# Output projection: where the first half's last twelve products stand among the second half's

## The chip, the cores and the metric

The kernel runs on one core of one Trainium2 chip. The time is the device time of one execution in microseconds, the median of three runs. Five engines work side by side, each through its own queue in order: TensorE (PE, the matrix products; its weight loads are shown apart as PEld), VectorE (DVE), ScalarE (ACT), GpSimd (POOL) and SyncE (SP, which here only issues DMAs).

## What is computed

One decoder block on 512 tokens of width 1024, in float32: a gated merge of an attention and a pooling branch, projected back by `w_out`, then an MLP. The part that matters here, cut from the reference:

```python
merged = gates[:, :, 0] * a + gates[:, :, 1] * p
x = x + (merged @ w_out[l]).astype(x.dtype)
h2 = rmsnorm(x, norm_mlp_g[l])
z = jnp.square(jax.nn.relu(h2 @ w_up[l]))
x = x + (z @ w_down[l]).astype(x.dtype)
```

## The kernel before

Every float32 product is made of three faster ones. A matrix is split into a high part (a rounded copy, written by ACT, line 112 for weights) and a low part (the difference, written by DVE, line 113), and high x high, high x low and low x high are summed in PSUM. So each weight tile costs a cast on ACT, then a subtract on DVE, before all its products can run.

The output projection takes `merged` (high part `vh`, low part `vl` in the profile, `mh` and `ml` in the code, in 8 slices `k` of 128 columns) times `w_out`, in two halves of 512 output columns. Each half has four weight tiles, and each tile serves two slices `k`. They are called o0_0 to o0_3 for the first half and o1_0 to o1_3 for the second; `wh_` and `wl_` are their high and low parts. The tokens are four row tiles of 128. A product of row tile t and slice k is three PE instructions of shape 128x512 (lines 588, 589, 590): `vh` x `wh`, `vh` x `wl`, `vl` x `wh`. Row tile t of the first half sums in PSUM bank po0_t, of the second half in po1_t. The profile drops the numbers and calls all of them po, wh_o, wl_o.

The high parts lie in a rotation of four buffers, so the high part of o1_3 goes where that of o0_3 was: its cast waits until the last product that reads o0_3 is done. Those products (slice k = 7 of the first half, twelve instructions) need the merge of the last attention head, which comes late. The low parts lie in four buffers of their own.

When a bank is complete, DVE adds it to the residual `x1` (line 594) and ACT sums the squares of the row (line 568). After the second half's add, a short chain on ACT and DVE (lines 578 to 582) makes the row's scale, line 645 writes the normalised row tile `h2`, and eight PE transposes (line 653) bring it into the layout of the up projection (banks h2T*t*). Their banks are split again into high and low (lines 665 and 666, tiles gab1 and gab2), which the first products of the up projection (lines 792, 795 and 798, banks um) read.

The kernel is written with a tile framework that orders the instructions of each engine itself: it runs its own cost model while it builds the program, and takes next what it reckons is ready. `after(later, earlier)` adds a rule of order without a semaphore: `later` may not be placed ahead of `earlier`. Without a rule, products of different banks may be mixed.

Of the kernel before, what the change touches and what calls it, by code (L numbers as in the profile page):

```python
# [21 lines left out]
NK = D // P  # L22
# [29 lines left out]
def block_kernel(ctx, tc, xT, x_tok, gains, pos, consts, w_in, w_v, w_pool, w_out, w_up, w_dn, out):  # L52
# [4 lines left out]
    def after(later, earlier):  # L57
        tc.add_manual_dep(
            later.ins, earlier.ins.name,
            mybir.DependencyInfo(mybir.DependencyClass.NoSync, mybir.DependencyReason.DATA), reason="issue order",  # L60
        )

    state = {}
# [8 lines left out]
    def bank(i, name):  # L72
        return ps.tile([P, S], F32, tag=f"b{i}", name=name)
# [16 lines left out]
    def f(ap):  # L90
        return ap.bitcast(F32)
# [24 lines left out]
    def get_w(src, name, eng=None, hold=None):  # L116
        raw, hi, lo = load_w(src, name)
        if eng == "dma":

            A.copy(out=hi, in_=raw)  # L120
            A.mul(out=lo, in_=f(hi), mul=-1.0)
            G.dma_start(out=lo, in_=src, accum_op=ALU.add)
        else:
            ins = split_w(raw, hi, lo, eng=eng)
            if hold:
                after(ins, hold)
        return hi, lo
# [91 lines left out]
    for n in range(2):  # L219
        accs = [bank((0, 1, 2, 3, 4, 5, 6, 0)[4 * n + t], f"v{n}_{t}") for t in range(NT)]  # L220
        for kk in range(4):
# [7 lines left out]
            for k2 in range(2):  # L229
# [4 lines left out]
                k = 2 * kk + k2  # L234
# [327 lines left out]
    def gain(g, i):  # L562
        nc.sync.dma_start(out=g, in_=gains[i])
        return g, A.mul(out=g, in_=g, mul=-0.5)
# [10 lines left out]
    def row_scale(t, n):  # L575

        src, r, u = (st[:, t, i : i + 1] for i in (n, 4, 5))
        A.activation(out=r, in_=src, func=AF.Ln, scale=1.0 / D, bias=st[:, t, 2:3])
        A.activation(out=r, in_=r, func=AF.Exp, scale=-0.5)
        state["rows"] = A.activation(out=u, in_=r, func=AF.Square, scale=1.0 / math.sqrt(D))  # L580
        V.scalar_tensor_tensor(out=u, in0=src, scalar=st[:, t, 3:4], in1=u, op0=ALU.add, op1=ALU.mult)
        V.scalar_tensor_tensor(out=r, in0=u, scalar=-3.0, in1=r, op0=ALU.add, op1=ALU.mult)
        return r

    def mm_rows(a_, t, k, w, start, stop):
        hi, lo = w
        sl, tsl = slice((k % 2) * 512, (k % 2) * 512 + 512), slice(t * P, t * P + P)
        m = T.matmul(a_, lhsT=mh[:, k, tsl], rhs=hi[:, sl], start=start, stop=False)
        T.matmul(a_, lhsT=mh[:, k, tsl], rhs=lo[:, sl], start=False, stop=False)
        return m, T.matmul(a_, lhsT=ml[:, k, tsl], rhs=hi[:, sl], start=False, stop=stop)  # L590

    def x1_add(t, n, a_):
        xs = x1[:, t, n * 512 : n * 512 + 512]
        V.tensor_tensor(out=xs, in0=a_, in1=xs, op=ALU.add)
        return square(t, n, R[t][:, 0:2, :].rearrange("p a t -> p (a t)"))

    def forms_h2(forms, x):

        w, u, a11, a12 = (h_[:, i, :, x] for h_ in (hw, h2f) for i in range(2))
        for form in forms:  # L600
            ins = None
            if form in (S2, S4):
                ins = V.scalar_tensor_tensor(out=w, in0=w, scalar=-1.0, in1=a11 if form == S2 else a12, op0=ALU.mult, op1=ALU.subtract)
            elif form == S3:
                ins = V.tensor_tensor(out=u, in0=a11, in1=u, op=ALU.subtract)
            if form in (S3, S4):
                after(ins, state[form - 1])
            hi, lo = (g_[:, :, x] for g_ in gf[form])
            A.copy(out=hi, in_=u if form == S3 else w)
            state[form] = V.tensor_tensor(out=lo, in0=u if form == S3 else w, in1=f(hi), op=ALU.subtract)  # L610

    po = [bank(t, f"po0_{t}") for t in range(NT)]
    for kk in range(4):
        w = get_w(w_out[0, kk], f"o0_{kk}", V if kk else "dma", state["scaled"] if kk > 1 else None)
        for k in (2 * kk, 2 * kk + 1):
            for t in range(NT):
                m, _ = mm_rows(po[t], t, k, w, k == 0, k == NK - 1)
                if k == 4:
                    after(m, state["pv"])
    for t in range(NT):  # L620
# [5 lines left out]
    g2b, _ = gain(R[4].rearrange("p b c -> p (b c)"), 0)  # L626
# [7 lines left out]
    for t in range(NT):  # L634
        a_ = bank(4 + t, f"po1_{t}")
        for k in range(NK):
            m, end = mm_rows(a_, t, k, ws[k // 2], k == 0, k == NK - 1)
            if t > 1 and k == 0:
                after(m, state["po"])
        if 0 < t < 3:  # L640
            for b in range(2):
                after(state["h2T", t - 1, b], end)
        state["po"] = end
        x1_add(t, 1, a_)
        state["h2", t] = V.scalar_tensor_tensor(out=h2[:, t % 2], in0=x1[:, t, :], scalar=row_scale(t, 1), in1=g2b, op0=ALU.mult, op1=ALU.mult)
        pv = []
        for b in range(2):
            pt = bank((t % 2) * 2 + b, f"h2T{t}_{b}")
            for j in range(4):
                k = 4 * b + j  # L650
                if j == 1:
                    state["h2T", t, b] = state["h2T"]
                state["h2T"] = T.transpose(out=pt[:, j * P : j * P + P], in_=h2[:, t % 2, k * P : k * P + P], identity=ident)
            pv.append(pt.rearrange("p (j q) -> p j q", q=P))
        sl = slice((t % 2) * P, (t % 2) * P + P)
        if t > 1:

            A.copy(out=hw[:, 1, :, sl], in_=pv[0])
            V.tensor_tensor(out=hw[:, 0, :, sl], in0=pv[1], in1=hw[:, 1, :, sl], op=ALU.subtract)
            forms_h2((S1, S2), sl)  # L660
        if t == 3:
            forms_h2((S3,), slice(0, HS))
        for b in range(t // 2, 2):
            hi, lo = (gab[b][:, t // 2, i, :, sl] for i in range(2))
            A.copy(out=hi, in_=pv[b])
            part = V.tensor_tensor(out=lo, in0=pv[b], in1=f(hi), op=ALU.subtract)
            if t == 3:
                after(part, state[S3])
            if t < 2:
                A.copy(out=h2f[:, b, :, sl], in_=pv[b])  # L670
# [371 lines left out]
```

## Time and profile before

| | |
|---|---|
| median of three runs | 672.47 us (672.26 to 672.51) |
| the profiled execution, its own time | 672.8 us |
| its span, first to last instruction | 671.0 us |
| so outside the span | 1.8 us |
| PE busy | 661.8 us, 99% of the span |
| DVE busy | 529.6 us, 79% |
| ACT busy | 467.5 us, 70% |
| PE's share of the chain of waits that ended last | 98% |

The output projection's products run from 297 to 348 us of the span, and the up projection follows at once. In the timeline, a row is a start in us, a duration in us, the engine and line, output <- inputs, a count, and in brackets the idle time ahead of it with what ended it. The end of a product is modelled: a 128x512 product shows 0.39 us, but the next one starts before that. "xN" at a row's end means N instructions merged, and the duration is then of all of them.

### The profile page before, as it was taken

Reading aid. Unit: us, or ns where it says so; the run is one execution under the profiler, and the core shown is the slowest. Engines: PE = TensorE matmul, PEld = TensorE weight load, DVE = VectorE, ACT = ScalarE, POOL = GpSimd, SP = SyncE. Lnnn points to the kernel's source line nnn. Section 1 sums busy time; section 2 is a strip of 40 time slices with the busy share of each in tenths; the row PEclk is TensorE's granted clock in tenths of the full one; section 3 lists DMA queues with packets and bytes.
Section 4 is the critical chain, followed back from the end, with each engine's and each line's share of the span. In section 5 each row is a group of like instructions: output and inputs, shape, how many; then the busy total and the mean of one; then the engine's idle time right before and its main releaser. Section 6 shows DMA issues by size and latency. Waiting matters only on the chain.

```text
span 671.0 us, 9986 instructions
## 1 busy us (share of the span) xinstructions
PE 661.8 (99%) x3680; PEld 578.3 (86%) x3680; DVE 529.6 (79%) x897; ACT 467.5 (70%) x756; POOL 91.1 (14%) x115
## 2 busy tenths in 40 slices
PE   9999999999999999999999999999999999999995
PEld 7888888888888888888789988999889998899884
DVE  6855977799979978795688999658993599747995
ACT  8465587979788688976477974368743695266974
POOL 2001110021012112300202020202102021211120
PEclk9999999999999999999999999999999999999998
DMA  9416474345254357454876596876959588584863
GB/s 320 155 60 188 123 153 126 87 123 113 95 133 127 95 132 151 104 174 178 283 203 115 165 228 184 174 207 132 235 195 194 183 163 260 132 199 135 211 126 126
DMA packets 32737, 108.82 MB, mean 162 GB/s; under 512 B 4016, under 2 KB 4912, under 8 KB 32688
## 3 DMA queue, kind: packets, MB, share of 16 engines
q0 software_dynamic: 10512, 38.28, 32.0%
q1 hardware_dynamic: 21744, 69.38, 29.4%
q8 instruction: 29, 0.48, 0.3%
q10 hardware_dynamic: 432, 0.52, 0.2%
q14 instruction: 20, 0.16, 0.1%
HBM read 106.07 MB, written 2.10 MB: 161 GB/s over the span
## 4 chain that ended last, share of the span: by engine, by line
PE 98%; DMA 1%; DVE 0%; ACT 0%; issue 0%; SPq 0%
PE um L795 8%; PE um L792 8%; PE um L798 8%; PE dm L885 8%; PE dm L887 8%; PE dm L888 8%; PE v L237 2%; PE o L420 2%; PE ga L134 2%; PE ga L133 2%; PE k L137 2%; PE ga L137 2%; PE gp L137 2%; PE k L134 2%; PE k L133 2%; PE gp L134 2%
## 5 line engine op out<-in xcount | busy, mean ns | idle before, releaser
L403 ACT ACTIVATE p<-p,st 128x128 f32<-128x128 f32 (+3 forms) x64 | 35.8, 561 | 19.8 <-DVE st L399 19.5
L887 PE MATMUL dm<-wh_dt,z 128*128 128x512 f32 (+1 forms) x128 | 49.5, 387 | 0.0
L888 PE MATMUL dm<-wl_dt,z 128*128 128x512 f32 (+1 forms) x128 | 49.4, 386 | 0.0
L885 PE MATMUL dm<-wh_dt,z 128*128 128x512 f32 (+1 forms) x128 | 49.0, 387 | 0.0
L795 PE MATMUL um<-gss,wh_ut 128*128 128x256 f32 x192 | 48.2, 283 | 0.0
L792 PE MATMUL um<-gss,wh_ut 128*128 128x256 f32 x192 | 48.0, 283 | 0.0
L905 DVE TENSOR_TENSOR x<-x,dm 128x512 f32<-128x512 f32 x48 | 32.5, 681 | 15.7 <-PE dm L888 15.6
L112 ACT CAST wh_ut<-wga_uNone 128x1024 fp32r<-128x1024 f32 x24 | 24.8, 1051 | 28.5 <-PE dm L887 19.9
L112 ACT CAST wh_ub<-wr_u 128x1024 fp32r<-128x1024 f32 x24 | 25.1, 1049 | 25.4 <-PE um L795 10.7
L113 DVE TENSOR_TENSOR wl_ut<-wga_uNone,wh_ut 128x1024 fp32r<-128x1024 f32 x24 | 29.0, 1221 | 12.7 <-ACT wh_ut L112 12.7
L887 PE MATMUL dm<-wh_db,z 128*128 128x512 f32 x96 | 37.2, 389 | 0.0
L888 PE MATMUL dm<-wl_db,z 128*128 128x512 f32 x96 | 37.2, 389 | 0.0
L795 PEld LDWEIGHTS um<-gss,wh_ut 128*128 128x128 f32 x192 | 36.9, 192 | 0.0
L792 PEld LDWEIGHTS um<-gss,wh_ut 128*128 128x128 f32 x192 | 36.8, 192 | 0.0
L885 PE MATMUL dm<-wh_db,z 128*128 128x512 f32 x96 | 35.7, 389 | 0.0
L113 DVE TENSOR_TENSOR wl_ub<-wr_u,wh_ub 128x1024 fp32r<-128x1024 f32 x24 | 29.1, 1219 | 8.4 <-ACT wh_ub L112 8.4
L112 ACT CAST wh_dt<-wga_dNone 128x1024 fp32r<-128x1024 f32 x24 | 24.9, 1050 | 14.9 <-issue 6.9
L694 POOL DMA_DIRECT2D wga_dNone<-w_dn x16 | 13.9, 868 | 154.2 <-DVE wl_dt L113 154.2
L765 DVE TENSOR_TENSOR z<-rawz,z 128x1024 fp32r<-128x1024 f32 x28 | 33.6, 1216 | 0.5 <-ACT z L762 0.5
L399 DVE CUSTOM_DVE_ANT_0 p<-s,mask 128x128 f32<-128x128 f32 (+3 forms) x64 | 30.6, 482 | 3.2 <-PE s L398 3.0
L795 PE MATMUL um<-gab,wh_ub 128*128 128x256 f32 x128 | 32.5, 283 | 0.0
L792 PE MATMUL um<-gab,wh_ub 128*128 128x256 f32 x128 | 32.4, 283 | 0.0
(322 smaller groups left out, 2174.4 us busy)
## 6 DMA issues: line engine op xcount, KB each, us to landing
wr_u<-w_up SPq DMA_DIRECT2D x24, 512.0 KB, 5.7
wr_d<-w_dn SPq DMA_DIRECT2D x24, 512.0 KB, 4.1
wga_uNone<-w_up POOLq DMA_DIRECT2D x18, 512.0 KB, 6.1
wga_dNone<-w_dn POOLq DMA_DIRECT2D x16, 512.0 KB, 5.7
wr_k<-w_in SPq DMA_DIRECT2D x8, 512.0 KB, 3.3
wr_ga<-w_in SPq DMA_DIRECT2D x8, 512.0 KB, 3.3
wr_gp<-w_in SPq DMA_DIRECT2D x8, 512.0 KB, 3.4
wl_ga<-w_in POOLq DMA_DIRECT2D x8, 512.0 KB, 5.4
```

The source lines that it names most:

```text
L112: ins = A.copy(out=hi[:, sl], in_=raw[:, sl])
L113: state["low"] = (eng or G).tensor_tensor(out=lo[:, sl], in0=raw[:, sl], in1=f(hi)[:, sl], op=ALU.subtract)
L134: T.matmul(acc, lhsT=hi[:, c], rhs=rl[k], start=False, stop=False)
L137: T.matmul(acc, lhsT=lo[:, c], rhs=rh[:, k, :], start=False, stop=k == NK - 1)
L403: A.activation(out=pr[:, c, :N], in_=pr[:, c, :N], func=AF.Exp, scale=-1.0, bias=st[:, c : c + 1], accum_out=st[:, 2 + c : 3 + c])
L765: lo = V.tensor_tensor(out=z[:, 1], in0=r, in1=f(z[:, 0]), op=ALU.subtract)
L792: m = T.matmul(a_, lhsT=hi[:, c], rhs=rh[:, k, :], start=p + k == 0 and onto is None, stop=False, skip_group_check=True)
L795: T.matmul(a_, lhsT=hi[:, c], rhs=rl[:, k, :], start=False, stop=False, skip_group_check=True)
L798: m = T.matmul(a_, lhsT=lo[:, c], rhs=rh[:, k, :], start=False, stop=k == 3, skip_group_check=True)
L885: m = T.matmul(a_, lhsT=zh, rhs=hi[:, sl], start=p == 0 and start, stop=False, skip_group_check=True)
L887: T.matmul(a_, lhsT=zl, rhs=hi[:, sl], start=False, stop=False, skip_group_check=True)
L888: end = T.matmul(a_, lhsT=zh, rhs=lo[:, sl], start=False, stop=p == 3, skip_group_check=True)
```

## The change

Two lines of order. `state["po"]` now holds, once the first half is written, the last product of its last bank. In the second half, row tile 0 may not begin slice k = 6 (the first that reads weight tile o1_3) until that product is placed. And the products of row tiles 1, 2 and 3 start only after those of the row tile ahead of them have all been placed; before, this held for row tiles 2 and 3 alone.

```diff
@@ -614,7 +614,7 @@
         w = get_w(w_out[0, kk], f"o0_{kk}", V if kk else "dma", state["scaled"] if kk > 1 else None)
         for k in (2 * kk, 2 * kk + 1):
             for t in range(NT):
-                m, _ = mm_rows(po[t], t, k, w, k == 0, k == NK - 1)
+                m, state["po"] = mm_rows(po[t], t, k, w, k == 0, k == NK - 1)
                 if k == 4:
                     after(m, state["pv"])
     for t in range(NT):
@@ -635,7 +635,7 @@
         a_ = bank(4 + t, f"po1_{t}")
         for k in range(NK):
             m, end = mm_rows(a_, t, k, ws[k // 2], k == 0, k == NK - 1)
-            if t > 1 and k == 0:
+            if t and k == 0 or not t and k == NK - 2:
                 after(m, state["po"])
         if 0 < t < 3:
             for b in range(2):
```

What this does to the order of PE around the end of the first half, first as it was. (In these rows po0 and po1 are the banks of the two halves, then the row tile; wh_o1_3 is the high part of the second half's last weight tile.)

```order
L589 MATMUL po0_3_3007<-wl_o0_3_3102,vh_113 128x512
L590 MATMUL po0_3_3007<-wh_o0_3_3101,vl_114 128x512
L590 MATMUL po1_1_3224<-wh_o1_1_3159,vl_114 128x512
L588 MATMUL po1_1_3224<-wh_o1_2_3165,vh_113 128x512
L589 MATMUL po1_1_3224<-wl_o1_2_3166,vh_113 128x512
L590 MATMUL po1_1_3224<-wh_o1_2_3165,vl_114 128x512
L588 MATMUL po1_1_3224<-wh_o1_2_3165,vh_113 128x512
L589 MATMUL po1_1_3224<-wl_o1_2_3166,vh_113 128x512
L590 MATMUL po1_1_3224<-wh_o1_2_3165,vl_114 128x512
L588 MATMUL po1_0_3175<-wh_o1_3_3171,vh_113 128x512
L588 MATMUL po1_1_3224<-wh_o1_3_3171,vh_113 128x512
L589 MATMUL po1_0_3175<-wl_o1_3_3172,vh_113 128x512
```

The first two rows end the first half. Seven products of row tile 1 stand between them and the first that reads o1_3, and two high-part products before the first that reads its low part. Ahead of these rows, 18 products of row tile 0 and 11 of row tile 1 stood mixed with the first half's last twelve: 41 products in all, up to and with the second row.

The same place now:

```order
L588 MATMUL po0_2_3006<-wh_o0_3_3101,vh_113 128x512
L589 MATMUL po0_2_3006<-wl_o0_3_3102,vh_113 128x512
L588 MATMUL po0_3_3007<-wh_o0_3_3101,vh_113 128x512
L589 MATMUL po0_3_3007<-wl_o0_3_3102,vh_113 128x512
L590 MATMUL po0_0_3004<-wh_o0_3_3101,vl_114 128x512
L590 MATMUL po0_1_3005<-wh_o0_3_3101,vl_114 128x512
L590 MATMUL po0_2_3006<-wh_o0_3_3101,vl_114 128x512
L590 MATMUL po0_3_3007<-wh_o0_3_3101,vl_114 128x512
L588 MATMUL po1_0_3175<-wh_o1_3_3171,vh_113 128x512
L589 MATMUL po1_0_3175<-wl_o1_3_3172,vh_113 128x512
L590 MATMUL po1_0_3175<-wh_o1_3_3171,vl_114 128x512
```

The twelve now follow the 18 products of row tile 0 directly (30 products up to the last of the first half, so it stands 11 earlier), their four `vl` products come together at the end, and the very next product reads o1_3. All 11 products of row tile 1 have moved behind row tile 0, with the rest of their row tile.

On DVE, the place at which the low part of o1_3 is made reads the same in both kernels:

```order
L594 TENSOR_TENSOR x1_2994<-po0_0_3004,x1_2994 128x512
L594 TENSOR_TENSOR x1_2994<-po0_1_3005,x1_2994 128x512
L594 TENSOR_TENSOR x1_2994<-po0_2_3006,x1_2994 128x512
L594 TENSOR_TENSOR x1_2994<-po0_3_3007,x1_2994 128x512
L113 TENSOR_TENSOR wl_o1_3_3172<-wr_o1_3_3169,wh_o1_3_3171 128x1024
L572 TENSOR_SCALAR st2_3003<-st2_3003 128x1
```

Nothing moved here: the subtract stands behind the four adds of the first half's banks.

Later on PE, a piece of the difference among row tile 2's products (the transposes of row tile 0's `h2`):

```order
 L589 MATMUL po1_2_3273<-wl_o1_2_3166,vh_113 128x512
 L590 MATMUL po1_2_3273<-wh_o1_2_3165,vl_114 128x512
+L653 MATMUL h2T0_0_3208<-ident_87,h2_2996 128x128 x4
+L653 MATMUL h2T0_1_3213<-ident_87,h2_2996 128x128 x4
 L588 MATMUL po1_2_3273<-wh_o1_3_3171,vh_113 128x512
 L589 MATMUL po1_2_3273<-wl_o1_3_3172,vh_113 128x512
```

Row tile 0's transposes moved forward by 19 places, from among row tile 3's products. Those of row tiles 1, 2 and 3 keep their place to within four rows. On ACT and DVE the chains of row tile 0 and row tile 1 (lines 568 to 645), which were interleaved, now stand one behind the other. No instruction is added or removed on any engine, and the orders of POOL and SP are unchanged.

## The prediction

> **What bounds the kernel now.** I read the page first (busy shares, the chain that ended last), then PE's waits over the whole run, then the timeline around the end of the first half. The page:
>
> ```profile
> span 671.0 us, 9986 instructions
> PE 661.8 (99%) x3680; PEld 578.3 (86%) x3680; DVE 529.6 (79%) x897; ACT 467.5 (70%) x756; POOL 91.1 (14%) x115
> PE 98%; DMA 1%; DVE 0%; ACT 0%; issue 0%; SPq 0%
> ```
>
> The waits of PE, in us, times, longest:
>
> ```profile
> PE warm L172 <- POOL eps L163: 1.1, 1, 1.1
> PE po L589 <- DVE wl_o L113: 0.4, 1, 0.4
> PE v L237 <- ACT wh_v L112: 0.3, 1, 0.3
> ```
>
> PE is the bound from end to end, and it idles three times. One idle, 0.4 us, is at the place of the change: the product that needs the low part of o1_3. So whatever makes PE wait here is paid in full at the end, for behind this place PE never waits and can give nothing back; and no new order can win more here than that wait.
>
> PE around it (a pair merged at 329.90: the last product of the first half, then one of row tile 1):
>
> ```profile
> 329.90 0.62 PE L590 MATMUL po<-wh_o,vl 128*128 128x512 f32 x2
> ...
> 331.71 0.61 PE L588 MATMUL po<-wh_o,vh 128*128 128x512 f32 x2
> 332.69 0.50 PE L589 MATMUL po<-wl_o,vh 128*128 128x512 f32 x1 [0.37 <-DVE wl_o L113]
> 333.03 0.40 PE L590 MATMUL po<-wh_o,vl 128*128 128x512 f32 x1
> ...
> 335.09 0.39 PE L588 MATMUL po<-wh_o,vh 128*128 128x512 f32 x1
> ...
> 342.35 0.39 PE L590 MATMUL po<-wh_o,vl 128*128 128x512 f32 x1
> ```
>
> The last two rows are the first and last of 33 in a row: 7.26 us / 32 = 0.227 us a product. ACT and DVE there:
>
> ```profile
> 325.43 1.06 ACT L564 ACTIVATE rawz<-rawz 128x1024 f32<-128x1024 f32 x1 [0.39 <-DMA rawz<-gains]
> 330.32 1.06 ACT L112 CAST wh_o<-wr_o 128x1024 fp32r<-128x1024 f32 x1 [3.83 <-PE po L590]
> 328.51 2.51 DVE L594 TENSOR_TENSOR x<-po,x 128x512 f32<-128x512 f32 x4 [2.22 <-PE po L590]
> 331.41 1.23 DVE L113 TENSOR_TENSOR wl_o<-wr_o,wh_o 128x1024 fp32r<-128x1024 f32 x1 [0.40 <-ACT wh_o L112]
> ```
>
> This is a chain: the first half's last product ends (329.90 + 0.39 = 330.29), the cast of o1_3 starts 0.03 later and ends at 331.38, the subtract ends at 332.64, the product starts at 332.69. From end of product to next product 2.40 us; nine products of the second half ran meanwhile, and hid all but the tail.
>
> **The change part by part.** *The wait that goes.* Behind the pair at 331.71 the next product was due at 331.71 + 2 x 0.227 = 332.16; it came at 332.69 (0.53 late), and the one behind it after 0.34 instead of 0.227 (0.11 more). Cost of the old wait: 0.64 us.
>
> *The wait that comes.* By the order, the last product of the first half stands 11 places earlier: 329.90 - 11 x 0.227 = 327.40, ending at 327.79. Nothing holds it up on the way: the last `vl` it reads is written at 323.33 (the row below), 3.4 us before its first use.
>
> ```profile
> 322.64 0.69 DVE L497 TENSOR_TENSOR vl<-o,vh 128x512 fp32r<-128x512 f32 x1 [0.69 <-ACT vh L496]
> 319.40 1.22 DVE L113 TENSOR_TENSOR wl_o<-wr_o,wh_o 128x1024 fp32r<-128x1024 f32 x1
> 320.54 0.68 DVE L484 TENSOR_TENSOR o<-o,y 128x512 f32<-128x512 f32 x1
> 345.88 1.88 DVE L666 TENSOR_TENSOR gab<-h2T,gab 128x512 fp32r<-128x512 f32 x3
> ```
>
> ACT is free from 326.49 (the 325.43 row), so the cast runs 327.82 to 328.88. All of the cover is gone: the next product reads this cast and the one after it the subtract, and behind these two on PE's queue stands everything else. The subtract has a second condition: it stands behind four adds, which are now released nearly together. The first add's product starts three steps before 327.40 and ends at 327.11, so it starts at 327.14 (0.03 later, as 328.51 followed a product's end). DVE instructions of this size follow one another every 0.60 us (the 345.88 row: 1.88 for three of 0.68 each), so the fourth starts at 328.94 and ends at 329.62. The next starts 0.08 before such an end (319.40 + 1.22 against 320.54): 329.54. The subtract ends at 330.77, and the L589 product starts 0.05 later, at 330.82. It was due at 327.40 + 2 x 0.227 = 327.85: 2.97 late, with the slow restart (0.11) 3.08 us. The profile would show this as about 1.1 us idle before L588 and 1.5 before L589.
>
> The sum: 3.08 - 0.64 = **+2.44 us**.
>
> *Bounds of that term.* Below: if the adds did not delay the subtract (it would start at 328.91 and end at 330.14), the product starts at 330.19, 2.34 late: 2.34 + 0.11 - 0.64 = +1.81. Above: if the adds run one behind the other without overlap (0.69 each, as the single rows show), +0.09 x 3 = +2.71. I take 2.44, since DVE rows of this size do follow at 0.60.
>
> *What moves behind the wait.* All later PE work shifts by 2.44 us, and so must what feeds it, or a second wait appears. The moved transposes of row tile 0 need its `h2`. The chain from a row tile's add to its `h2`, alone in the queues:
>
> ```profile
> 348.41 0.68 DVE L594 TENSOR_TENSOR x<-po,x 128x512 f32<-128x512 f32 x1
> 349.19 1.29 DVE L645 SCALAR_TENSOR_TENSOR h<-x,st,rawz 128x1024 f32<-128x1024 f32 x1
> 351.12 1.28 DVE L645 SCALAR_TENSOR_TENSOR h<-x,st,rawz 128x1024 f32<-128x1024 f32 x1
> ```
>
> The last row is row tile 3's: 351.12 + 1.28 - 348.41 = 3.99 us (349.19 is row tile 2's, used further down). Bank po1_0 is now complete five products into the restart, 330.82 + 0.11 + 4 x 0.227 + 0.39 = 332.2; plus 3.99 and one 1.05 us weight cast that now stands in the chain on ACT: 337.3. The transposes come 47 products after that L589, at 341.6: a margin of 4.3 us. Row tile 1's bank is complete at 337.7, its `h2` at 341.7, its transposes at 347.0. Costed at nothing. Tighter is the low part of `h2` for the up projection's first products:
>
> ```profile
> 345.29 1.03 PE L653 MATMUL h2T<-ident,h 128*128 128x128 f32 x8
> 347.88 0.31 PE L795 MATMUL um<-gab,wh_ub 128*128 128x256 f32 x1
> 353.06 1.03 PE L653 MATMUL h2T<-ident,h 128*128 128x128 f32 x8
> 391.35 1.21 DVE L765 TENSOR_TENSOR z<-rawz,z 128x1024 fp32r<-128x1024 f32 x1
> 395.29 0.62 PE L885 MATMUL dm<-wh_dt,z 128*128 128x512 f32 x2
> ```
>
> Today the third L666 ends at 345.88 + 1.88 = 347.76, 0.12 before L795 reads it. After the change, three more products stand between row tile 1's transposes and L795 (about 3.3 us instead of 2.59), so this margin widens to some 0.7, unless DVE is behind a weight subtract. Costed at nothing, with its price below. Row tile 2's transposes have 2.6 us of room today (353.06 - 350.48), and its chain shifts with PE. Much later the order swaps a weight subtract (1.14 us) with the split of `z`: today that split ends at 392.56, and the first product of that `z` starts at 395.29, so 1.6 us remain. Costed at nothing. The earlier `h2` of row tile 0 gains nothing either: PE never waited for it.
>
> The span becomes 671.0 + 2.44 = 673.4, the profiled time 672.8 + 2.44 = 675.2; the median stands 0.3 below that execution, so 672.47 + 2.44 = **674.9 us**, 0.36% more. Three runs span 0.25 us; under 0.2% (1.3 us) a difference counts as none.
>
> **The rivals.** *Not slower: the cover remains.* The releaser of the cast is inferred. If its buffer were free before the twelve end, and the subtract not behind the adds, only ACT would hold it: cast from 326.49, subtract done at 326.49 + 1.06 + 0.03 + 1.23 = 328.81, product at 328.86, 1.01 late: 1.01 + 0.11 - 0.64 = +0.5, 672.9. It decides if the cast begins by 326.5. For it: only that releasers are inferred. Against: 0.03 us between product's end and cast, and the adds ahead on DVE's queue. Faster than 671.8 (no wait at all, -0.64) has no source, as PE idles nowhere else behind.
>
> *A second wait at L795.* If one weight subtract (1.14 us pitch, 320.54 - 319.40) slips in ahead of row tile 1's L666, 0.7 of margin leaves 0.4 to 0.5 of wait: 675.4.
>
> *The clock falls in the pause.* The granted clock, in windows of 1 us at the end (last columns: PEclk, DMA share, GB/s), PE's last product being over at 663.6:
>
> ```profile
> 666.00:667.00 1.00, 0.00 (x0) 0.00 (x0) 0.65 (x1) 0.64 (x2) 0.00 (x0) 1.00 0.72 281
> 667.00:668.00 1.00, 0.00 (x0) 0.00 (x0) 0.00 (x0) 0.00 (x0) 0.00 (x0) 0.57 0.98 373
> 668.00:669.00 1.00, 0.00 (x0) 0.00 (x0) 0.00 (x0) 0.00 (x0) 0.00 (x0) 0.50 0.95 369
> ```
>
> It halves some 3.5 us into idleness. The new pause has two idle pieces of 1.1 and 1.5 us with a product between, so the clock should stay at 1.00. If it fell all the same, and for as long as it took to fall, 3.5 us at half rate lose 1.75: 674.9 + 1.75 = 676.7. The Trainium skill (TensorE: Matmul & The Clock Gate, Part 1: The HAM clock gate) says that a whole free-running window of about 3.4 us without work drops the array's clock to half, and a busy one restores it. By that rule nothing is added here, and one window lost would cost an estimated 1.7 us, 676.6. The windows above agree with it.
>
> **How the numbers follow.** The forecast, a pause between the bounds (+1.81 to +2.71): 0.78. Second wait: 0.07. Clock: 0.05. Cover remains: 0.05. A mishap that I don't see, of either sign: 0.05. Slower: 0.78 + 0.07 + 0.05 + 0.01 = 0.91; same 0.05 + 0.02 = 0.07; faster 0.02. The range runs from 674.3 (lower bound) less 0.1 for the spread of runs to the second wait on the upper bound, 672.47 + 2.71 + 0.5 = 675.7, plus 0.1: 674.2 to 675.8; it leaves out cover and clock.
>
> **What would show it.** Right: the cast of o1_3 near 327.8; PE idle for o1_3 in two pieces, 2.6 us in all instead of 0.37; the subtract starting right behind the fourth add, 0.6 us after the cast is done; row tile 0's transposes without a wait; PEclk 1.00 from 330 to 336; PE's sum of busy time unchanged. Wrong: the cast starting before the fourth `vl` product ends (cover), a PE wait on L795 or L653 (second wait), a product pitch above 0.227 behind the pause (clock), or less than 2 us of idle time with a span that grows all the same.

## The result, and the profile after

The median of six executions is 677.0 us (674.6 to 679.1), against 672.7 us (672.3 to 673.7) for six of the kernel before on the same chip. The ratio is 1.0057, with a 95% interval of 1.0046 to 1.0069. The change is slower, as forecast; but by 4.3 us, where 2.4 were forecast, and outside the range. The six times are also far apart: 674.61 and 675.40 on one side, 676.72, 677.29, 677.43 and 679.14 on the other. The first two show a mean granted clock of 0.998 over the execution, the others 0.993 to 0.995.

The profiled execution is the 679.14 us one. First two lines of its page and the two waits of PE that the change concerns (us, times, longest):

```profile
span 677.3 us, 9984 instructions
PE 665.4 (98%) x3680; PEld 580.6 (86%) x3680; DVE 529.6 (78%) x897; ACT 468.7 (69%) x756; POOL 91.3 (13%) x115
...
PE po L589 <- DVE wl_o L113: 1.4, 1, 1.4
...
PE po L588 <- ACT wh_o L112: 1.1, 1, 1.1
```

The pause has come as forecast, in two pieces of 1.1 and 1.4 us. But PE's busy time has also grown, from 661.8 to 665.4 us, with the same 3680 products: some of them ran longer. The timeline of PE (start, duration in us) shows which:

```profile
328.98 1.07 PE L590 MATMUL po<-wh_o,vl 128*128 128x512 f32 x4
331.19 0.50 PE L588 MATMUL po<-wh_o,vh 128*128 128x512 f32 x1 [1.14 <-ACT wh_o L112]
333.08 0.51 PE L589 MATMUL po<-wl_o,vh 128*128 128x512 f32 x1 [1.39 <-DVE wl_o L113]
...
333.88 0.59 PE L589 MATMUL po<-wl_o,vh 128*128 128x512 f32 x1
334.26 0.63 PE L590 MATMUL po<-wh_o,vl 128*128 128x512 f32 x1
...
337.25 0.43 PE L588 MATMUL po<-wh_o,vh 128*128 128x512 f32 x1
```

(This execution began 2.2 us late, which is taken up at the end; all times here are later by that.) From 334.26 to 337.25 the products follow at 0.427 us instead of 0.227. The granted clock, in windows of 1 us (last three columns: PEclk, DMA share, GB/s), says why:

```profile
333.00:334.00 1.00, 0.92 (x4) 0.79 (x5) 0.61 (x9) 0.60 (x2) 0.26 (x2) 0.96 0.85 246
334.00:335.00 1.00, 1.00 (x4) 0.81 (x3) 0.07 (x1) 0.00 (x0) 0.71 (x1) 0.50 1.02 205
...
337.00:338.00 1.00, 1.00 (x6) 0.78 (x5) 0.00 (x0) 1.00 (x2) 0.00 (x0) 0.84 1.04 274
...
671.00:672.00 1.00, 0.00 (x0) 0.00 (x0) 0.55 (x2) 0.94 (x4) 0.00 (x0) 0.92 0.02 8
```

A window of 1 us at 0.96 was at half rate for 0.08 us, so the clock fell at 333.92; 0.84 means 0.32 us, so it was back at 337.32, 3.40 us later. The last row is the kernel's end, where PE has nothing more to do: the clock falls there at 671.84. ACT and DVE in the pause:

```profile
330.09 1.05 ACT L112 CAST wh_o<-wr_o 128x1024 fp32r<-128x1024 f32 x1 [1.36 <-PE po L590]
329.41 2.48 DVE L594 TENSOR_TENSOR x<-po,x 128x512 f32<-128x512 f32 x4 [0.89 <-PE po L590]
331.81 1.22 DVE L113 TENSOR_TENSOR wl_o<-wr_o,wh_o 128x1024 fp32r<-128x1024 f32 x1
```

The cast starts as the last product of the first half is done, and the subtract 0.08 us before the fourth add ends, 0.67 us after the cast. That is the chain that was forecast.

### The profile page after: what moved, and what is told of

The parts are those of the page before. It is cut to its first block, busy times and chain, and to the rows that moved or that the text cites. A ratio compares the mean times of both kernels' runs of the same rounds, so it can differ in the third digit from the quotient of the medians.

```text
span 677.3 us, 9984 instructions
## 1 busy us (share of the span) xinstructions
PE 665.4 (98%) x3680; PEld 580.6 (86%) x3680; DVE 529.6 (78%) x897; ACT 468.7 (69%) x756; POOL 91.3 (13%) x115
## 4 chain that ended last, share of the span: by engine, by line
PE 96%; DMA 1%; DVE 1%; ACT 0%; SPq 0%; issue 0%
PE um L798 8%; PE um L795 8%; PE um L792 8%; PE dm L885 7%; PE dm L887 7%; PE dm L888 7%; PE v L237 2%; PE v L238 2%; PE o L420 2%; PE v L239 2%; PE ga L134 2%; PE ga L133 2%; PE k L137 2%; PE ga L137 2%; PE gp L137 2%; PE k L134 2%
## 5 line engine op out<-in xcount | busy, mean ns | idle before, releaser
L795 PE MATMUL um<-gss,wh_ut 128*128 128x256 f32 x192 | 48.2, 283 | 0.0
L795 PEld LDWEIGHTS um<-gss,wh_ut 128*128 128x128 f32 x192 | 36.9, 192 | 0.0
L795 PE MATMUL um<-gab,wh_ub 128*128 128x256 f32 x128 | 32.5, 283 | 0.0
```

Source lines behind the costliest of these rows:

```text
L795: T.matmul(a_, lhsT=hi[:, c], rhs=rl[:, k, :], start=False, stop=False, skip_group_check=True)
```

## The experiments

**Theory A.** The change costs the pause (+2.4 us), and in most executions, on top of it, a stretch at half clock that the pause sets off. **Theory B.** The clock's fall in this one profile is incidental; the time beyond +2.4 us comes from elsewhere, such as the start of the execution.

Of the change's two rules the second alone (row tile 1 behind row tile 0) gives every engine the order of the changed kernel, and the first alone (slice 6 of row tile 0 behind the first half) leaves the old order; so the two were not run apart.

### The changed kernel again

No edit.

> The changed kernel once more, for the spread of its time. Theory A (the clock falls in the pause of some executions): two kinds of execution, about 675.0 us with a mean granted clock of 0.998 and about 677.2 with 0.994 or 0.995, the second in about two of three. Theory B (the time beyond +2.44 us comes from the start of an execution, where the first weights landed 0.6 us later in the profiled one): times spread between 674.6 and 679.2 without a second value of the clock that goes with them.

The ratio is 1.0052 (1.0039 to 1.0065). Two executions with a clock of 0.998 took 674.71 and 675.38 us; four with 0.991 to 0.995 took 676.94, 676.95, 676.98 and 678.18. The second value of the clock goes with the longer time in every one of them, which speaks for A. It does not yet say which causes which.

### The pause kept, but filled

```diff
+            if not t and k == NK - 2:
+                fill, prev = bank(7, "fill"), state["po"]
+                for _ in range(5):
+                    d = T.matmul(fill, lhsT=mh[:, 0, 0:P], rhs=ws[0][0][:, 0:512], start=True, stop=True)
+                    after(d, prev)
+                    prev = d
...
+                m = T.matmul(a_, lhsT=mh[:, k, 0:P], rhs=hi[:, 0:512], start=False, stop=False)
...
+                for _ in range(6):
...
-            if t and k == 0 or not t and k == NK - 2:
+            if t and k == 0:
```

> The changed kernel with eleven extra products in the pause: five before the product that waits for the cast of o1_3 and six between it and the product that waits for the subtract. They write a bank whose content is then overwritten. Eleven times 0.227 us is 2.5 us, as long as the pause, so PE is busy there but the cast and the subtract come no earlier. Theory A: the pause's 2.44 us stay, the clock doesn't fall: 674.9 us (674.4 to 675.4) in every execution, clock 0.998. Theory B: the spread is as in the changed kernel, median near 677, up to 679.

The eleven extra products land in the pause, and the chain behind it keeps its times. PE, then ACT and DVE:

```profile
326.60 1.07 PE L590 MATMUL po<-wh_o,vl 128*128 128x512 f32 x4
327.51 1.29 PE L640 MATMUL fill<-wh_o,vh 128*128 128x512 f32 x5
328.82 0.50 PE L644 MATMUL po<-wh_o,vh 128*128 128x512 f32 x1
329.15 1.56 PE L648 MATMUL fill<-wh_o,vh 128*128 128x512 f32 x6
330.70 0.51 PE L651 MATMUL po<-wl_o,vh 128*128 128x512 f32 x1
327.71 1.05 ACT L112 CAST wh_o<-wr_o 128x1024 fp32r<-128x1024 f32 x1 [1.39 <-PE po L590]
329.43 1.22 DVE L113 TENSOR_TENSOR wl_o<-wr_o,wh_o 128x1024 fp32r<-128x1024 f32 x1
```

The product that waits for the subtract starts 4.10 us after the four-product row, as in the changed kernel (333.08 - 328.98). All five executions lie between 674.97 and 675.82 us; the median is 675.15, against 676.94 for the changed kernel on the same chip. Eleven products of useless work make the kernel 1.8 us faster, because PE is not idle. Theory B would have left the spread. (The mean clock of four of the five is 0.996, and that value alone marks no fall in the pause: the half clock behind PE's last product counts in it too. In the first profile after the change, 5.5 us of it there (671.84 to 677.3) and 3.4 us at the pause make 1 - 0.5 x 8.9 / 677.3 = 0.993. Only the 675.15 us execution was profiled; its clock reads 1.00 around the pause.) What stays, 675.15 against 673.07 of the kernel before, is the pause, 2.1 us by these medians.

### Only the first piece filled

The same edit with the six products left out.

> The changed kernel with five of the extra products only, ahead of the product that waits for the cast. One idle piece of 1.4 us is left in front of the product that waits for the subtract. The fall of the clock by a share of idleness in a window of 3.41 us (falls were seen at 2.0 us and more idle in one window, none at 1.47): no fall, 675.0 us (674.5 to 675.6) in every execution. If any idle piece of over 1 us can set the fall off, wherever it lies: about 676.7 in more than half of the executions.

The five executions took 674.64 to 676.08 us, median 675.45, and the profile (the 675.01 us one) shows 1.4 us of idleness at that product and a clock of 1.00 throughout. There, one piece of 1.4 us set nothing off. The two longest, 675.72 and 676.08, lie above what was expected and were not profiled. The kernel before alone ranged from 672.29 to 674.19 here, but a fall in these two is not ruled out.

### A longer pause

```diff
         split_w(raw, hi, lo)
+        if kk == 3:
+            V.tensor_tensor(out=lo, in0=raw, in1=f(hi), op=ALU.subtract)
```

> The changed kernel with the subtract that makes the low part of o1_3 done a second time; the second product of o1_3 waits for that one, which stands behind six short instructions of DVE: the second idle piece grows from 1.4 to about 2.9 us. Theory A: now every position of the windows has one with 2 us idle, so all executions lie in one group: 675.0 + 1.5 + 1.2 to 1.7 for the half rate (less where part of that window is idle) = 677.7 to 678.3, and none near 676.5. If the fall hangs on something else than the idle time, two groups stay, 676.5 and 678.2.

One group, as A has it, though higher than expected: 679.39, 679.61 and 679.65 us, and one of 681.16. PE's waits:

```profile
PE po L589 <- DVE wl_o L632: 2.9, 1, 2.9
...
PE po L588 <- ACT wh_o L112: 1.1, 1, 1.1
```

The second piece is the 2.9 us that was expected. Of the 1.3 us that the estimate missed, 0.4 is a new wait of PE far behind (`PE um L794 <- ACT rawz L822`), and 0.6 lies behind PE's last product; I did not follow these further. By the mean clocks, 0.992 to 0.995, no execution escaped the half clock; only the 679.61 us one was profiled. Four are few: if nine in fifteen fall, as they do without this edit, four in a row come by chance once in eight times. The 681.16 us execution, at 0.992, stays unexplained.

### Where the fall is decided: three more profiles

No edit.

> The changed kernel, one profile more, for the place of the windows. The falls so far lie on a grid of 3.413 us with the fall at the kernel's end (99, 100 and 94 periods between the two). If that grid decides: with a grid line in the last 0.7 us of the pause's second idle piece or up to 1 us behind it, the window ahead of the line holds 2.0 us idle or more, and the clock falls on the line; with the line in the first 0.4 us of the first piece or up to 0.8 us ahead of it, the window behind the line does, and the clock falls one period later; with the line between these, each window holds under 1.5 to 1.9 us, and it doesn't fall.

> As the look before: a fall on the grid line if one window of 3.413 us holds 2.0 us idle or more (about 676.7 us), none if both neighbours hold less than 1.5 (about 675.0 us); between these the bound itself is measured.

> As the two looks before, a third place of the grid: a fall (676.7 us) where one window holds 2.0 us idle or more, none (675.0 us) where both hold less than 1.5.

They took 675.03, 675.31 and 677.73 us. In each profile the fall at the kernel's end was read as above: 670.29, 670.78 and 671.04. The falls of three earlier profiles give the step of the grid: they lie 337.93, 341.34 and 320.86 us ahead of the fall at the kernel's end. These differ by 3.41 us and by five times that, and are 99, 100 and 94 times 3.413. Counting back in such steps gives the line of the grid nearest the pause: 328.96, 329.45 and 329.71. The pause is the same in all three, so only its place on the grid differs. In the first two the line lies between the pieces, no period holds more than 1.40 us of idleness, and the clock didn't fall, as expected. In the third the period ahead of the line holds 1.74 us, between the two bounds of the expectation, and the clock fell at 329.71, on the line. PE and the clock in the periods on both sides of the line; each fence is one kernel, the second column is PE's busy time:

```profile
325.55:328.96 3.41, 2.28 (x10) 1.50 (x8) 2.45 (x5) 2.00 (x3) 1.17 (x2) 1.00 1.02 412
328.96:332.37 3.41, 2.01 (x9) 1.49 (x9) 2.47 (x11) 2.14 (x8) 2.20 (x3) 1.00 0.96 279
```

```profile
326.30:329.71 3.41, 1.67 (x7) 0.81 (x5) 2.88 (x5) 2.21 (x6) 2.32 (x3) 1.00 1.00 392
329.71:333.12 3.41, 2.63 (x6) 2.15 (x7) 1.40 (x10) 1.30 (x5) 1.13 (x2) 0.50 0.99 235
333.12:336.53 3.41, 3.41 (x9) 2.64 (x9) 0.93 (x3) 2.26 (x6) 0.00 (x0) 0.50 1.05 262
```

The first is 675.03 us long: 2.28 and 2.01 us busy of 3.41 (67 and 59%), and the clock stays. The second is 677.73: after a period with 1.67 us busy (49%) the clock halves for the next. That next one, with 0.78 us of the pause in it, is 77% busy, and the clock stays down for another. A period that was busy throughout brings it back: from 336.53 it reads 1.00. Two periods at half rate are why this execution took 677.73 us where a fall was expected to give 676.7. The same reading of the first profile after the change, of the one in the run "again", and of the longer pause:

```profile
330.50:333.91 3.41, 1.33 (x5) 0.89 (x6) 3.11 (x12) 3.10 (x9) 2.08 (x4) 1.00 0.93 329
333.91:337.32 3.41, 3.41 (x10) 2.64 (x9) 0.69 (x1) 1.54 (x5) 0.80 (x1) 0.50 1.02 215
```

```profile
327.33:330.74 3.41, 1.21 (x5) 0.42 (x3) 3.35 (x5) 2.67 (x6) 2.31 (x3) 1.00 1.03 399
330.74:334.16 3.42, 3.10 (x7) 2.48 (x8) 1.41 (x10) 0.84 (x4) 1.15 (x2) 0.50 1.02 222
```

```profile
328.77:332.18 3.41, 0.50 (x1) 0.19 (x1) 3.41 (x12) 2.46 (x9) 2.08 (x3) 1.00 1.09 329
```

All three fell, after 39, 35 and 15%. From the first two of these lines to the falls at the kernels' ends it is 99 periods (671.84 - 333.91 = 337.93 = 99 x 3.413) and 100 (672.08 - 330.74 = 341.34).

### The four adds behind the subtract

```diff
-        V.tensor_tensor(out=xs, in0=a_, in1=xs, op=ALU.add)
+        state["add", t, n] = V.tensor_tensor(out=xs, in0=a_, in1=xs, op=ALU.add)
...
+    for t in range(NT):
+        after(state["add", t, 0], state["low"])
```

> The changed kernel with the four adds of the first half ordered behind the subtract of o1_3 on DVE (the lower bound of the pause's term, +1.81 us). The second idle piece shrinks from 1.39 to 0.76 us: 674.3 us where the clock stays. The idle time is 1.9 us in all, between the most that was seen without a fall in one window (1.47) and the least with one (2.01). If the bound lies near 2 us: no falls, all at 674.3 (up to 675.0). If it lies nearer to 1.5: a fall in up to half of the executions, those near 676.0.

The second piece shrank to 0.76 us, as the lower bound of the prediction's term has it. Two executions kept the clock (0.998) and took 674.80 and 675.32 us; three took 676.71 to 677.02, with 0.995 and 0.996, and by times and clocks together these fell, as the second case of the expectation has it. Only the 674.80 us one was profiled. That 1.9 us of idleness is enough where one period holds it fits with the 1.74 us above. The 0.6 us that the pause lost came back only in part. The first product of the up projection that reads a low part, 0.11 us behind the product ahead of it in the first of the three profiles above, is now 0.42 behind: the second wait of the prediction, 0.3 us in size. It appears where PE arrives earlier (349.38 against 349.96) and DVE's split begins later (349.06 against 348.78), behind a weight subtract.

```profile
349.38 0.28 PE L794 MATMUL um<-gab,wh_ub 128*128 128x256 f32 x1
349.80 0.39 PE L797 MATMUL um<-gab,wh_ub 128*128 128x256 f32 x1
```

### The cast freed of its wait

The high part of o1_3 gets a buffer of its own, so that its cast need not wait for the first half. The first try put it into the buffer that later holds part of the transposed `h2`:

```diff
...
+        if own:
+            hi = big.tile([P, 2, 1024], F32R, tag="s1a", name=f"wh_{name}")[:, 0]
+        else:
+            hi = wp.tile([P, 1024], F32R, tag="wh", name=f"wh_{name}", bufs=4)
...
+        raw, hi, lo = load_w(w_out[1, kk], f"o1_{kk}", own=kk == 3)
```

> The changed kernel, but the high part of o1_3 goes into a buffer of its own, so that its cast needn't wait for the end of the first half. The order of PE stays that of the change. If the pause (by whichever theory) is nothing but this cast and subtract, it goes, with the old wait of 0.64 us too: 672.5 - 0.6 = 671.8 us, clock 0.998, no idle of PE at o1_3. If the new order itself costs time elsewhere (transposes of row tiles 0 and 1, a second wait further down), it stays above 673.

> The kernel before with the same own buffer for the high part of o1_3. Only the old wait goes: 672.5 - 0.64 = 671.8 us. With the changed kernel under the same edit it should agree within 0.3 us, if the order of PE's products is worth nothing by itself.

Both missed: 677.42 us for the changed kernel with it, 675.79 for the one before, where 671.8 was expected. The pause at o1_3 is gone (0.2 us left), but the transposed `h2` can't be written until the last product that reads o1_3 is done, so PE waits at the up projection. The waits of the changed kernel with this buffer:

```profile
PE um L795 <- ACT gab L668: 1.2, 1, 1.2
...
PE um L798 <- DVE gab L669: 0.9, 1, 0.9
PE po L592 <- DVE wl_o L116: 0.2, 1, 0.2
```

I had moved the wait, not removed it. It still tells something: at this other place, with other products, the clock fell again. In the period ahead of the fall PE was busy for 1.39 us of 3.41 (41%); in the profile of the kernel before with this buffer the two periods held 2.69 and 1.94 us (79 and 57%), and it didn't fall:

```profile
346.83:350.24 3.41, 1.39 (x6) 0.69 (x4) 3.34 (x6) 2.81 (x7) 0.00 (x0) 1.00 0.85 306
350.24:353.65 3.41, 3.34 (x15) 3.34 (x16) 2.26 (x5) 2.91 (x7) 0.00 (x0) 0.50 0.00 1
```

```profile
345.18:348.59 3.41, 2.69 (x16) 1.95 (x14) 2.58 (x5) 1.74 (x4) 0.00 (x0) 1.00 0.86 315
348.59:352.00 3.41, 1.94 (x14) 1.75 (x15) 1.80 (x4) 3.38 (x11) 0.00 (x0) 1.00 0.06 22
```

The second of these profiles is of an execution of 676.08 us. Two others of the same kernel took 677.75 and 677.76 us with a mean clock of 0.995; they were not profiled, but the clock probably fell there.

The second try takes a buffer that nothing needs before the first `z`:

```diff
...
-        hi = wp.tile([P, 1024], F32R, tag="wh", name=f"wh_{name}", bufs=4)
+        hi = own or wp.tile([P, 1024], F32R, tag="wh", name=f"wh_{name}", bufs=4)
...
-        raw, hi, lo = load_w(w_out[1, kk], f"o1_{kk}")
+        raw, hi, lo = load_w(w_out[1, kk], f"o1_{kk}", own=zf("wo3")[:, 0].rearrange("p b c -> p (b c)") if kk == 3 else None)
```

> The changed kernel with the high part of o1_3 in a buffer of its own again, now in one that nothing needs before 390 us (the first buffer used for this delayed the transposed h2 of row tiles 0 and 1). No pause at o1_3 (its subtract stands ahead of the four adds), none at the first up projection: 672.9 (the kernel before on that chip) less 0.6 = 672.3 us, no fall. If the order of the changed kernel costs something beside the pause, it stays above 673.

> The kernel before with the same own buffer. The subtract of o1_3 stands behind three of the four adds, but the product that needs it comes later here: the old wait of 0.64 us goes, 672.3 us against 672.9 of the kernel before on that chip. It would be the same as that kernel if a new wait at the first up projection eats it.

The changed order with it takes 672.49 us, the kernel before 672.84: a ratio of 0.9998 (0.9990 to 1.0007). (One of its eleven executions took 674.63 us, the others at most 673.15.) Both the pause and the half clock are gone, and 4 us with them, so the order of the products as such costs nothing beyond the noise; against the kernel before nothing that can be measured is won. PE's whole list of waits is now:

```profile
PE warm L172 <- POOL eps L163: 1.1, 1, 1.1
PE po L589 <- DVE wl_o L113: 0.2, 1, 0.2
```

The old order with the same buffer takes 674.29 us (ratio 1.0020, 1.0011 to 1.0028), a miss by 2 us. It has no wait at o1_3 either, but a new one, `PE um L795 <- DVE gab L666`, of 1.0 us. On DVE the framework has placed row tile 2's normalisation between the low parts of the transposed `h2`:

```profile
345.76 0.69 DVE L666 TENSOR_TENSOR gab<-h2T,gab 128x512 fp32r<-128x512 f32 x1
346.36 1.28 DVE L645 SCALAR_TENSOR_TENSOR h<-x,st,rawz 128x1024 f32<-128x1024 f32 x1
...
348.24 1.28 DVE L666 TENSOR_TENSOR gab<-h2T,gab 128x512 fp32r<-128x512 f32 x2
```

Taking away one wait let the framework choose another order, and with it another wait. The rest of its loss I did not follow. No version tried beats the kernel before.

## Why the prediction was wrong, and where it was right

**The pause, +2.44 us: right.** The prediction's chain holds step by step: the cast behind the last product, the subtract behind the fourth add, two pieces of 1.1 and 1.4 us (2.6 forecast, 2.53 measured). The kernel before and the first of the three profiles, which kept its clock, give its price. First the old kernel's first product of `v` and its last product, then the changed kernel's:

```profile
5.54 1.20 PE L237 MATMUL v<-wh_v,xh 128*128 128x512 f32 x4 [0.33 <-ACT wh_v L112]
663.34 0.28 PE L888 MATMUL dm4b<-wl_dt,z 128*128 128x256 f32 x1
```

```profile
5.30 1.20 PE L237 MATMUL v<-wh_v,xh 128*128 128x512 f32 x4 [0.21 <-ACT wh_v L112]
665.51 0.28 PE L888 MATMUL dm4b<-wl_dt,z 128*128 128x256 f32 x1
```

665.51 - 5.30 - (663.34 - 5.54) = +2.41 us. PE's busy sum is unchanged there, 661.9 us against 661.8. The six executions of the changed kernel with a clock of 0.998, of fifteen in all, took 674.61 to 675.40 us, mean 675.07; 674.9 was forecast.

**The clock: wrong, and this is the step that failed.** "The new pause has two idle pieces of 1.1 and 1.5 us with a product between, so the clock should stay at 1.00." It fell in nine of the fifteen, by their times and clocks (the three of these nine that were profiled show it). Its price, 1.6 us and more, is most of what lies between the 674.9 us forecast and the 677.0 measured. I had read the fall at the end of the old kernel, 3.5 us into idleness, as the need of so much unbroken idleness. That row could not show this: there the whole period ahead of the fall was empty (663.7 to 667.1 us, PE busy 0.00), so it says nothing of a period that is half empty. Nor was the rival's 0.05 founded on any row with a pause in it. The Trainium skill (TensorE: Matmul & The Clock Gate, Part 1: The HAM clock gate) gives a free-running window of 3413 ns and says that the clock halves after at least one idle window. On the first the traces agree: the falls here lie on just such a grid. On the second they do not: periods in which PE was 15 to 49% busy were enough, and the measurement decides.

**The price of a fall: right for one period at half rate.** The rival was worked out as 3.5 us at half rate, +1.75. From the product that waits for the subtract to the kernel's last product it is 665.51 - 330.58 = 334.93 us in the first of the three profiles, and 669.62 - 333.08 = 336.54 in the first one after the change: +1.61. Where the grid splits the pause so that two periods run at half rate (the 677.73 us one), it is 668.22 - 330.49 = 337.73, +2.8.

**No second wait: right** for the changed kernel; no wait on L795 or L653 shows in any of its five profiles. It is a real neighbour, though: it came with 0.3 us where the adds were moved, and with 1.0 us where the buffer was freed in the old order.

**The cover remains: refuted.** In the profile after, ACT stood idle for 1.4 us and began the cast 0.04 us after the last product of the first half ended.

The chance of slower, 0.91, stood on the pause alone and was borne out. The range was too narrow, since it left out the clock's rival, which adds to the pause.

## What to carry to other kernels

A new wait on an engine that is the bound costs its length, and on PE perhaps 1.6 to 2.8 us more: add up the idle time within any 3.4 us instead of looking for the longest piece. When PE must wait there, short useless products in the gap can be cheaper than silence (1.8 us here). Before freeing a buffer or moving an instruction, look up who needs the new buffer next and what the framework will then place differently: a wait taken away at one point came back at the next with the adds moved, with the first buffer (in both orders), and with the second buffer in the old order.

## What the runs showed of the hardware

The granted clock of PE changes only on a grid of 3.41 us that runs on from the pause to the end of the kernel (94, 99 and 100 periods between two falls of one execution). At the waits it halved after each of five periods in which PE was 15 to 49% busy, and after none of those with 57% or more. It came back after periods that were 91 to 100% busy, and stayed down after one with 77%.

These shares give no sharp bound. At the end of the changed order with the second buffer, a period with PE 48% busy left the clock at 1.00; it fell one period later, at 669.17, after an empty one:

```profile
662.34:665.76 3.42, 1.65 (x14) 1.44 (x12) 2.04 (x8) 2.75 (x13) 0.00 (x0) 1.00 0.13 50
665.76:669.17 3.41, 0.00 (x0) 0.00 (x0) 1.13 (x3) 1.25 (x3) 0.00 (x0) 1.00 0.77 294
```

The ends of products are modelled, so an idle piece may be shown too short, and the period after which the clock fell at 49% has two such pieces. Counted only to the earliest start of the next product (0.227 us for 128x512, 0.12 for 128x256), that period is an estimated 36% busy and this one 44%. The end of the first profile after the change, where the clock fell after a period shown 43% busy, stands at 39% by the same count. This way of counting was chosen after the fact, and no run tests it.

So a pause's price depends on where the grid happens to lie, and one profile shows only one of its outcomes.

Most of the late start of the first profile after the change is of the same kind. Of the 2.2 us, 0.6 is a later first product of `v` (6.18 against 5.54); the other 1.6 is half rate. Its products follow at 0.42 us (8.48 to 8.90) until 9.71, and 671.84 less 194 periods is 9.65:

```profile
8.48 0.63 PE L239 MATMUL v<-wh_v,xla 128*128 128x512 f32 x1
8.90 0.63 PE L238 MATMUL v<-wl_v,xh 128*128 128x512 f32 x1
...
9.71 0.62 PE L238 MATMUL v<-wl_v,xh 128*128 128x512 f32 x2
```

The granted clock's column shows 1.00 there all the same, so at a kernel's start the pitch of the products is the better witness. Why some executions start at half rate and others not was not tried.
